# Trunk layer on one core: the q, k, v, o and z projections as seven half-size products (Strassen's scheme), all heads ahead of attention

## The chip, the cores and the metric

The kernel runs on one core of one Trainium2 chip. The metric is device time in microseconds (us) of one execution; lower is better. The median of three runs of the kernel before is 2274.1 us.

## The reference, cut to what matters

One layer of a hybrid trunk, for 1024 prompt tokens and for 32 sample tokens (8 sequences of 4), model width 1024. The part that the change touches is the product of the normalised rows with the columns of `w_in` that give q, k, v, o and z (each 2048 columns, four heads of 512), and the chunkwise attention that reads them:

```python
h = rmsnorm(x, norm_w)
pool_in, pool_z, qk_pre, v, o_pre, m_z, if_pre, gate_pre = jnp.split(h @ w_in, SPLIT_OFFSETS, axis=-1)
...
qk, conv_hist_new = causal_conv_silu(qk_pre, conv_hist, conv_w, conv_b)
q, k = jnp.split(qk, 2, axis=-1)
hc, c, n, m = mlstm_chunkwise(heads(q), heads(k) * (HEAD_DIM ** -0.5), heads(v), ...)
hc = hc * jax.nn.sigmoid(o_pre)
hc = head_rmsnorm(hc, mlstm_norm_w)
bm = (hc * jax.nn.silu(m_z)) @ w_mlstm_down
g_a, g_b = jnp.split(jax.nn.sigmoid(gate_pre), 2, axis=-1)
x = x + (g_a * a + g_b * bm) @ w_out
```

`mlstm_chunkwise` runs, for each head, over eight chunks of 128 tokens; from chunk to chunk it carries a 512 x 512 memory `C` (with one more column for the normaliser). The outputs are the layer's rows and all its new states.

## The kernel before

Every float32 product is made of three products of split operands: an operand x becomes `hi` (rounded, by ACT, L75 and L77) and `lo` = x - `hi` (by DVE, L81 and L83), and `mm3` (L88 to L90) adds hi x hi, hi x lo and lo x hi on PE.

The order of the work is as follows.

1. `norm_in` normalises the rows and leaves them feature-major as `hh` and `hl`, 1056 tokens wide (1024 of the prompt, then the 32 of the sample).
2. `head_gemm(h)`, for the four heads in turn, makes the products. For q and k the weights stand and the tokens move in three chunks of 352 columns (`fm`, 24 matmuls for a tile of 128 features and a chunk); `qk_tile` then does the causal convolution (three DVE operations, L488), silu, and a store to DRAM. For v, o and z the tokens stand and 256 weight columns move (`tok_group`). The sample's 32 rows take part in the q and k products as moving columns; for v, o and z they are separate float32 matmuls (`few`, L129). `load_w` loads 512 KB of weights at a time into `wraw` (2 buffers) and splits them into `whi` and `wlo` (3 buffers each).
3. `attn(h)` is a generator of eight `attn_step`s. While `head_gemm(h+1)` is written out, `tick` takes a step of it after each unit of product, at a rate of 0.45. So a head's attention is traced between the next head's products. The gates of all heads run in the same way beside head 0's products.
4. The last head's attention, and then `sample` (32 parts, each loads and stores 1 MB of state `ct`), run beside the merge gates (`merge_gates`, products of `hh` with the `gate_pre` columns) and the pool branch (`pool_branch`), at rates of 1.0 and 1.5. Then follow the down projections, `w_out` and the tail.

One `attn_step` of a middle chunk does on PE: 4 score matmuls (L605), 4 transposes of k (L629), 6 matmuls of the weighted scores with v and 24 of q with `C` (both into `num`), 24 for the new memory (eight groups of three into `kv`, which has two buffers), and 4 transposes of the result (L662). On DVE it does: `vlo`, the gated q (`t2k`, L618), `ql`, the decayed scores `p` (L607), `pl`, `kl`, eight updates of `C` (L642), four `Cl` (the split of the new `C`), and `den` (L651), its reciprocal (L652), the row sum `rs_ms` (L96), and the two products on the result (L654, L659): 23 operations. `Ch` and `Cl`, the split memory that the 24 q matmuls of the next chunk read, have one buffer each. The first chunk of a head has no q matmuls (and no gated q and no `ql`); the last makes no `Ch` and `Cl`. The loads of a step (`qk`, `v`, `dg`, `o`, `zz`) are issued by SP.

The kernel is built by a scheduler that sets the order of the instructions within each engine's queue from the traced program; an engine then runs its queue strictly in that order, and waits on semaphores.

```python
            self.feed(self.attn(h), 0.45)
...
        self.feed(rest(), RATE_A)
        self.merge_gates(range(5))
```

Of the kernel before, what the change touches and what calls it, by code (L numbers as in the profile page):

```python
# [18 lines left out]
P = 128  # L19
D = 1024  # L20
T = 1024          # prompt tokens
DB, DS = 8, 4     # sample batch, sample tokens
# [7 lines left out]
CW = NT // 3      # token chunk of the feature-major products  # L30
# [3 lines left out]
PH = 15           # pooling history  # L34
# [12 lines left out]
RATE_G, RATE_A, RATE_S = 0.8, 1.0, 1.5  # L47


class Trunk:  # L50
# [5 lines left out]
    # ---------------------------------------------------------------- helpers  # L56
# [35 lines left out]
    def rstd(self, pool, ss, n, rows=P):  # L92
        """(ss / n + eps) ** -0.5, one value per partition"""
        nc = self.nc
        ms = self.t(pool, [P, 1], "rs_ms", bufs=3)
        nc.vector.tensor_scalar(out=ms[:rows], in0=ss, scalar1=1.0 / n, scalar2=EPS, op0=ALU.mult, op1=ALU.add)  # L96
        r = self.t(pool, [P, 1], "rs_r", bufs=3)
        nc.gpsimd.tensor_tensor(out=r[:rows], in0=ms[:rows], in1=self.mhalf[:rows], op=ALU.pow)  # L98
        return r[:rows]

    def load_w(self, ap, n, scale=None):
        """rows of a weight, 256 columns at most: list of (hi, lo) for each k-tile"""
# [3 lines left out]
        for k0 in range(0, kt, 4):  # L106
            kk = min(4, kt - k0)
            raw = self.t(self.wp, [P, 4, 256], "wraw", bufs=2)
# [15 lines left out]
    def few(self, ps, rows, w):  # L124
        """NS rows (feature-major tiles, float32) times a weight: four partial sums, one per column group"""
# [5 lines left out]
    def sum4(self, out, ps, pool, groups=4):  # L131
        """sum of the partial sums of few()"""
# [9 lines left out]
    def fm(self, w, f, mov, consume, chunks=range(3)):  # L142
        """out[f-tile, tokens]: the weights stand, the activations (list of (hi, lo) [P, NT]) move"""
# [13 lines left out]
    def feed(self, gen, rate):  # L157
        """trace gen alongside the products: rate of its parts for each unit of product"""
# [16 lines left out]
    # ---------------------------------------------------------------- phase A  # L175
    def consts(self):
# [7 lines left out]
        nc.vector.memset(self.ones, 1.0)  # L184
        self.vc = self.t(c, [P, 72 + P], "vcols")
        self.nw = self.vc[:, 0:8]

    def columns(self):
        """per-feature vectors as columns"""
# [6 lines left out]
        v1 = self.t(self.ap_, [64, P], "v1")  # L196
        for o, n, name in ((8, 8, "ple_norm_w"), (16, 8, "pool_scale"), (24, 16, "mlstm_norm_w"), (40, 32, "conv_b")):
            nc.sync.dma_start(v1[o - 8:o - 8 + n, :], I[name].rearrange("(a b) -> a b", b=P))
        v2 = self.t(self.ap_, [P, P], "v2")
# [6 lines left out]
    def masks(self):  # L206
        nc, c = self.nc, self.cp
        one = self.t(self.ap_, [P, P], "one")
        nc.gpsimd.memset(one, 1.0)
        tri = self.t(self.ap_, [P, P], "tri")    # 1 where t >= s  # L210
# [14 lines left out]
        self.sel = self.t(c, [P, NS], "sel")     # 1 where the partition is t modulo 32  # L225
        nc.vector.tensor_reduce(out=self.sel, in_=self.ident.rearrange("p (g t) -> p t g", g=4), axis=AX.X,
                                op=ALU.add)
        # 1 / min(t + 1, 16)
        cnt = self.t(self.ap_, [P, 16], "cnt")
# [4 lines left out]
    def histories(self):  # L234
        """the rows before the convolution, feature-major"""
        nc, I, c = self.nc, self.I, self.cp
        self.chist = self.t(c, [P, 32, 24], "chist")
        h1 = self.t(self.ap_, [24, 2 * M], "h1")
        nc.sync.dma_start(h1, I["state_conv"].rearrange("b j f -> (b j) f"))
        for f0 in range(0, 32, 16):  # L240
            ps = self.mmps()
            for f in range(16):
                nc.tensor.transpose(ps[:, f * 24:(f + 1) * 24], h1[:, (f0 + f) * P:(f0 + f + 1) * P],
                                    self.ident[:24, :24])
            nc.vector.tensor_copy(self.chist[:, f0:f0 + 16, :], ps[:, :384].rearrange("p (f r) -> p f r", r=24))

    def norm_in(self):
# [3 lines left out]
        hp = self.hp  # L251
# [4 lines left out]
        v0 = None  # L256
        for i0, n in ((0, 3), (3, 3), (6, 3)):
            xs = []
            for i in range(i0, i0 + n):
                rows = P if i < 8 else NS  # L260
                x = self.t(self.ap_, [P, D], "x", bufs=6)
                nc.sync.dma_start(x[:rows], I["x_prompt"][i * P:(i + 1) * P, :] if i < 8 else I["x_sample"])
                xs.append((x, rows))
            if v0 is None:
                v0 = self.t(self.ap_, [8, P], "v0")
                nc.sync.dma_start(v0, I["norm_w"].rearrange("(a b) -> a b", b=P))
                ps = self.mmps()
                nc.tensor.transpose(ps[:, :8], v0, self.ident[:8, :8])
                nc.vector.tensor_copy(self.nw, ps[:, :8])
            for i, (x, rows) in enumerate(xs, i0):  # L270
                junk = self.t(self.ap_, [P, D], "xj", bufs=2)
                ss = self.t(self.ap_, [P, 1], "xss", bufs=3)
                if i % 3 == 1:
                    nc.vector.scalar_tensor_tensor(out=junk[:rows], in0=x[:rows], scalar=1.0, in1=x[:rows],
# [985 lines left out]
```

## Time and profile before

| what | value |
| --- | --- |
| runs of the kernel | 2271.71, 2274.1, 2277.27 us; median 2274.1 |
| the profiled execution | span 2277.1 us, 3.0 above the median |
| PE busy | 2235.1 us, 98% of the span, 16282 matmuls |
| DVE busy | 1121.0 us, 49% |
| ACT busy | 853.4 us, 37% |
| POOL busy | 126.4 us, 6% |
| traffic with HBM | 135 GB/s over the span |

PE, DVE, ACT and POOL are the four compute engines, SP issues the DMAs, PEld is PE's weight load. "Busy" is time in which an instruction was under way. A matmul's duration contains its drain, and the next one starts before it ends; so the price of a matmul in a stream is the distance from its start to the next one's start.

### The profile page before, as it was taken

The page shows a single profiled execution, that of the slowest core. Times are in us where ns is not written, and L with a number is a line of the kernel's source. Part 1 is how long each engine was busy: PE and PEld are TensorE (multiplying, and loading weights), DVE is VectorE, ACT ScalarE, POOL GpSimd, SP SyncE. Part 2 cuts the span into 40 slices and gives each one's busy share as a digit, 9 for nine tenths or more (in the row PEclk, how much of TensorE's full clock was granted, in tenths as well). Part 3 has the DMA queues.
Part 4 walks back from the last instruction along what each step waited for, and adds up shares of the span by engine and source line. Part 5 has one row for each costly group of instructions (what it writes and reads, how often), then busy time and mean ns, then how long its engine had stood idle before and what let it go on. Part 6 is the DMA issues. An engine that isn't in the chain of part 4 may idle for free.

```text
span 2277.1 us, 39798 instructions
## 1 busy us (share of the span) xinstructions
PE 2235.1 (98%) x16282; PEld 2137.3 (94%) x16282; DVE 1121.0 (49%) x2143; ACT 853.4 (37%) x1707; POOL 126.4 (6%) x380
## 2 busy tenths in 40 slices
PE   7999999999999999999999999999999999999998
PEld 6989999999999999999999998877878999999998
DVE  6551157444475343764434554567554234543545
ACT  5552255333354333553333332222233331223443
POOL 2120011000010000100000000000000000000100
PEclk8999999999999999999999999999999999999999
DMA  4353333344343344334444443777678333323112
GB/s 139 105 158 114 102 105 112 116 127 131 108 125 119 107 124 132 122 115 123 116 140 120 137 128 106 237 268 256 247 264 290 127 109 117 104 86 123 52 47 82
DMA packets 249866, 309.81 MB, mean 136 GB/s; under 512 B 14726, under 2 KB 187102, under 8 KB 249660
## 3 DMA queue, kind: packets, MB, share of 16 engines
q1 hardware_dynamic: 249684, 307.27, 42.3%
q8 instruction: 128, 2.10, 0.4%
q14 instruction: 54, 0.44, 0.1%
HBM read 198.17 MB, written 109.40 MB: 135 GB/s over the span
## 4 chain that ended last, share of the span: by engine, by line
PE 91%; DMA 5%; DVE 2%; ACT 1%; issue 1%; SPq 0%; DVEq 0%; POOL 0%; POOLq 0%; ACTq 0%
PE mm L88 25%; PE mm L89 25%; PE mm L90 25%; PE mm L129 2%; PE num L88 2%; PE num L89 2%; PE num L90 2%; PE num L774 1%; PE kv L88 1%; PE kv L90 1%; PE kv L89 1%; DMA ct<-state_mlstm_C 1%; PE misc L605 1%; DMA new_C_sample<-ct 1%; PE kv L778 1%; DMA draw<-hcD 1%
## 5 line engine op out<-in xcount | busy, mean ns | idle before, releaser
L88 PE MATMUL mm<-hh,whi 128*128 128x352 f32 x1536 | 502.8, 328 | 5.1 <-ACT whi L75 3.9
L89 PE MATMUL mm<-hl,whi 128*128 128x352 f32 x1536 | 499.1, 325 | 0.0
L90 PE MATMUL mm<-hh,wlo 128*128 128x352 f32 x1536 | 497.4, 325 | 0.0
L89 PE MATMUL mm<-wlo,hh 128*128 128x256 f32 x1536 | 433.0, 282 | 0.0
L88 PE MATMUL mm<-whi,hh 128*128 128x256 f32 x1536 | 432.6, 283 | 0.0
L90 PE MATMUL mm<-whi,hl 128*128 128x256 f32 x1536 | 430.8, 281 | 0.0
L81 DVE TENSOR_TENSOR wlo<-wraw,whi 128x1024 fp32r<-128x1024 f32 (+1 forms) x136 | 162.6, 1196 | 350.5 <-ACT whi L75 347.8
L88 PEld LDWEIGHTS mm<-hh,whi 128*128 128x128 f32 x1536 | 291.1, 190 | 15.9 <-ACT whi L75 4.2
L89 PEld LDWEIGHTS mm<-hl,whi 128*128 128x128 f32 x1536 | 292.1, 190 | 6.1 <-issue 5.0
L90 PEld LDWEIGHTS mm<-hh,wlo 128*128 128x128 f32 x1536 | 291.1, 190 | 6.2 <-issue 5.0
L88 PEld LDWEIGHTS mm<-whi,hh 128*128 128x128 f32 x1536 | 288.2, 188 | 8.6 <-ACT ph L75 4.9
L90 PEld LDWEIGHTS mm<-whi,hl 128*128 128x128 f32 x1536 | 290.2, 189 | 0.0
L89 PEld LDWEIGHTS mm<-wlo,hh 128*128 128x128 f32 x1536 | 288.3, 188 | 0.0
L75 ACT ACTIVATE whi<-wraw 128x1024 fp32r<-128x1024 f32 (+1 forms) x136 | 140.3, 1032 | 210.9 <-PE mm L89 98.1
L488 DVE SCALAR_TENSOR_TENSOR acc<-z,vcols,acc 128x352 f32<-128x352 f32 (+1 forms) x288 | 168.6, 590 | 81.0 <-ACT acc L486 75.5
L642 DVE SCALAR_TENSOR_TENSOR C<-C,dec,kv 128x258 f32<-128x258 f32 x224 | 102.0, 478 | 78.2 <-PE kv L90 77.1
L779 DVE SCALAR_TENSOR_TENSOR ct<-ct,dec,kv 128x512 f32<-128x512 f32 x128 | 91.8, 744 | 95.0 <-PE kv L778 94.1
L90 PE MATMUL mm<-mvhB,wlo 128*128 128x352 f32 x384 | 122.9, 321 | 0.3 <-DVE wlo L83 0.3
L88 PE MATMUL mm<-mvhB,whi 128*128 128x352 f32 x384 | 122.7, 323 | 0.4 <-ACT whi L77 0.3
L89 PE MATMUL mm<-mvlB,whi 128*128 128x352 f32 x384 | 122.9, 321 | 0.0
L98 POOL TENSOR_TENSOR rs_r<-rs_ms,cst 128x1 f32<-128x1 f32 (+1 forms) x60 | 38.8, 647 | 1058.1 <-DVE rs_ms L96 1021.4
L81 DVE TENSOR_TENSOR Cl<-C,Ch 128x516 fp32r<-128x516 f32 x112 | 77.7, 693 | 30.0 <-ACT Ch L75 27.8
(333 smaller groups left out, 4042.8 us busy)
## 6 DMA issues: line engine op xcount, KB each, us to landing
wraw<-w_in SPq DMA_DIRECT2D x112, 512.0 KB
ct<-state_mlstm_C SPq DMA_DIRECT2D x32, 1024.0 KB
new_C_sample<-ct SPq DMA_DIRECT2D x32, 1024.0 KB
qkD<-qkout SPq DMA_DIRECT2D x32, 512.0 KB
qk<-qkD SPq DMA_DIRECT2D x32, 512.0 KB
sgD<-sz SPq DMA_DIRECT2D x16, 528.0 KB
sg<-sgD SPq DMA_DIRECT2D x16, 528.0 KB
x<-x_prompt SPq DMA_DIRECT2D x16, 512.0 KB
```

Source lines behind the costliest of these rows:

```text
L75: self.nc.scalar.activation(out, in_, AF.Copy)
L81: self.nc.vector.tensor_tensor(out=out, in0=in_, in1=hi.bitcast(F32), op=ALU.subtract)
L88: mm(ps, lhsT=sh, rhs=mh, start=start, stop=False)
L89: mm(ps, lhsT=sh, rhs=ml, start=False, stop=False)
L90: mm(ps, lhsT=sl, rhs=mh, start=False, stop=stop)
L98: nc.gpsimd.tensor_tensor(out=r[:rows], in0=ms[:rows], in1=self.mhalf[:rows], op=ALU.pow)
L129: self.nc.tensor.matmul(ps[g, :], lhsT=rows[:, k, :], rhs=w[k][2], start=k < 4, stop=k >= kt - 4)
L488: nc.vector.scalar_tensor_tensor(out=acc[:, :tot], in0=z[:, o:o + tot], scalar=wc(o), in1=acc[:, :tot], op0=ALU.mult, op1=ALU.add)
L605: nc.tensor.matmul(ps[:, :L], lhsT=qk[:, 4 + d, :], rhs=qk[:, d, :], start=d == 0, stop=d == 3)
L642: nc.vector.scalar_tensor_tensor(out=self.C[:, d, x, :n], in0=self.C[:, d, x, :n], scalar=self.dec[:, h * NCH + c, 0:1], in1=kv[:, :n], op ...
L774: nc.tensor.matmul(num[32 * d:32 * d + 32, 0, :], lhsT=qm[:, b * P + d * NS:b * P + (d + 1) * NS], rhs=ct[:, d, :], start=b == 0, stop=b = ...
L779: nc.vector.scalar_tensor_tensor(out=ct[:, d, :], in0=ct[:, d, :], scalar=self.dec[:, h * DB + b, 1:2], in1=kv, op0=ALU.mult, op1=ALU.add)
```

## The change

q, k, v, o and z of one head are now made in blocks of 512 columns (20 blocks in all). The 1024 prompt tokens, the 1024 rows of the weight and the 512 columns are each cut in half; the block is then a 2 x 2 by 2 x 2 product of matrices, which takes eight half-size products in the plain way and seven by Strassen's scheme (in Winograd's form), with sums of operands ahead and sums of results behind.

- `norm_in` also builds the sums of the token side, once for all blocks: `T3`, `M2` and `N4` (each 4 tiles of 128 x 512, split), and it leaves a sum `M1` in the late half of `hh` and `hl`. `plain_h` puts the plain rows back there after the last block, since the merge gates and the pool branch read them. The callback `first` places the first two half products of the first block between the two halves of `norm_in`.
- `split_block` makes the seven half products. For each block DVE adds four pairs of weight tiles (128 x 1024), and does two `s2` adds, two negated adds and six adds in `put`; ACT copies two banks to `s1`. Seven weight tiles are split in place of four.
- In a half product (`half_product`) of q or k, 24 matmuls move 512 token columns each; of v, o or z, 48 matmuls move 256 weight columns each. The counts over the kernel: 2304 matmuls of 352 columns become 1344 of 512; 4608 of 256 become 4032.
- The sample's rows are separate float32 matmuls for all five kinds now (`few_part`, 16 for a block, 320 in all, where 192 were for v, o and z), with 32 small sums for q and k.
- The convolution of a tile runs over 512 and 568 columns in place of 352, 352 and 376.
- `run` traces all 20 blocks first, then the gates, and then the attention of all heads and the sample, at a rate of 2.6 (2.1 for the sample), beside the merge gates. What of the attention is left after seven of the eight groups of merge gates is traced on its own.

The diff, cut to its core:

```diff
-RATE_G, RATE_A, RATE_S = 0.8, 1.0, 1.5
+RATE_A, RATE_S = 2.6, 2.1
+HT = T // 2
...
+    def half_product(self, banks, w, act, tok, start, stop):
+        (wh, wl), (ah, al) = w, act
+        mm = self.nc.tensor.matmul
+        for j, ps in enumerate(banks):
...
+                for k in range(4):
+                    for n, (st, mv) in enumerate(((sh, mh), (sh, ml), (sl, mh))):
+                        mm(out, lhsT=st[k], rhs=mv[k], start=start and opens and k == 0 and n == 0,
+                           stop=stop and k == 3 and n == 2, skip_group_check=True)
+    def split_block(self, w, c0, tok, to, stage=None, held=None):
...
+            self.half_product(a, self.split_w(r11), self.early[0], tok, True, False)
...
+                nc.scalar.activation(s1[-1], x, AF.Copy)
+            self.half_product(a, self.split_w(r12), self.early[1], tok, False, True)
...
+        add(x3, r11, r21)
+        add(r21, r21, r22)
+        add(r11, r11, r21)
+        b = two()
+        self.half_product(b, self.split_w(r11), ops["M2"], tok, True, False)
...
+        add(r12, r12, r11)
+        self.half_product(b, self.split_w(x3), ops["T3"], tok, False, True)
...
+        self.half_product(c, self.split_w(r22), ops["N4"], tok, True, True)
...
+        self.half_product(d, self.split_w(r21), ops["M1"], tok, True, False)
...
+        self.half_product(d, self.split_w(r12), ops["B22"], tok, False, True)
...
-            self.feed(self.attn(h), 0.45)
...
+        for h in range(H):
+            for kind in "qvkoz":
+                self.block(h, kind, held.pop() if held else None)
+        self.plain_h()
...
+            yield from gates
...
+            for h in range(H):
+                yield from self.attn(h)
...
-        self.merge_gates(range(5))
+        self.merge_gates(range(7))
+        while not _s:
+            next(self.bg)
```

How the change moves instructions shows at two places of the queues.

On PE, in the attention of a head: before, the eight groups of `kv` stand between matmuls (`mm`) of the next head's products. This is a piece of head 0's attention in the queue of before:

```order
L88 MATMUL mm_3990<-hh_135,whi_3697 128x352
L89 MATMUL mm_3990<-hl_136,whi_3697 128x352
L88 MATMUL kv_3896<-vhi_421_3087,kh_3880 128x258
L89 MATMUL kv_3896<-vlo_422_3088,kh_3880 128x258
L90 MATMUL kv_3896<-vhi_421_3087,kl_3881 128x258
L88 MATMUL kv_3901<-vhi_421_3087,kh_3880 128x256
L89 MATMUL kv_3901<-vlo_422_3088,kh_3880 128x256
L90 MATMUL kv_3901<-vhi_421_3087,kl_3881 128x256
L90 MATMUL mm_3990<-hh_135,wlo_3698 128x352
L88 MATMUL mm_4026<-hh_135,whi_3691 128x352
```

And this is PE's queue of the change where a step of head 1 ends and the next begins (L833 are the transposes of the result, L776 the scores, L800 the transposes of k; `ph`, `pl` are the weighted scores):

```order
L90 MATMUL kv_11663<-vlo_1238_9501,kh_11618 128x256
L91 MATMUL kv_11663<-vhi_1237_9500,kl_11619 128x256
L833 MATMUL misc_11683<-ident_112,t2k_11674 128x128 x4
L776 MATMUL misc_11704<-qk_11691 128x128 x4
L800 MATMUL misc_11752<-ident_112,qk_11691 128x128 x4
L89 MATMUL num_11715<-vhi_1237_9500,ph_11711 128x258
L90 MATMUL num_11715<-vlo_1238_9501,ph_11711 128x258
L91 MATMUL num_11715<-vhi_1237_9500,pl_11712 128x258
L89 MATMUL num_11715<-vhi_1237_9500,ph_11711 128x256
```

The `mm` rows are gone from it. From its row 7150 to its row 8449, PE's queue holds the 24 steps of heads 1, 2 and 3, one after the other, and no matmul of any other work; the 14 tiles of the first seven groups of merge gates (1008 matmuls) stand ahead of them, around the gates and the eight steps of head 0.

On DVE, in the attention of a middle chunk: before, the operations of the step stand among weight splits (`wlo`) and the convolution (`acc`) of the next head:

```order
L642 SCALAR_TENSOR_TENSOR C_3092<-C_3092,dec_1206,kv_10876 128x258
L642 SCALAR_TENSOR_TENSOR C_3092<-C_3092,dec_1206,kv_10881 128x256
L618 TENSOR_TENSOR t2k_11190<-qk_11159,dg_11163 128x512
L81 TENSOR_TENSOR wlo_11423<-wraw_11420,whi_11422 128x1024
L81 TENSOR_TENSOR Cl_3094<-C_3092,Ch_3093 128x516
L81 TENSOR_TENSOR ql_11193<-t2k_11190,qh_11192 128x512
L488 SCALAR_TENSOR_TENSOR acc_11026<-z_11019,vcols_134,acc_11026 128x376
L642 SCALAR_TENSOR_TENSOR C_3092<-C_3092,dec_1206,kv_10888 128x258
L642 SCALAR_TENSOR_TENSOR C_3092<-C_3092,dec_1206,kv_10893 128x256
L488 SCALAR_TENSOR_TENSOR acc_11026<-z_11019,vcols_134,acc_11026 128x376
```

Now only operations of the attention stand there (L813 updates `C`, L830 is the last product on the result, `t2k` on L789 is the gated q; the last five rows belong to the next chunk, except the `Cl` between them, the fourth of this one):

```order
L830 SCALAR_TENSOR_TENSOR t2k_12650<-t2k_12650,rs_r_12656,zz_12536 128x512
L813 SCALAR_TENSOR_TENSOR C_9505<-C_9505,dec_9163,kv_12634 128x258
L813 SCALAR_TENSOR_TENSOR C_9505<-C_9505,dec_9163,kv_12639 128x256
L82 TENSOR_TENSOR Cl_9507<-C_9505,Ch_9506 128x516
L82 TENSOR_TENSOR vlo_1238_9501<-v_12749,vhi_1237_9500 128x2x256
L789 TENSOR_TENSOR t2k_12778<-qk_12747,dg_12751 128x512
L82 TENSOR_TENSOR Cl_9507<-C_9505,Ch_9506 128x516
L778 SCALAR_TENSOR_TENSOR p_12765<-misc_12760,dg_12751 128x128
L82 TENSOR_TENSOR ql_12781<-t2k_12778,qh_12780 128x512
L82 TENSOR_TENSOR pl_12768<-p_12765,ph_12767 128x128
```

What moved: the weight splits and the convolution are ahead of all of it, and a step's `vlo`, gated q, `p`, `ql` and `pl` stand behind the last updates of `C` of the step before.

## Rows read from the trace of the kernel before

**Rows 1.** The page: busy time, share of the span and instructions of each engine.

```profile
PE 2235.1 (98%) x16282; PEld 2137.3 (94%) x16282; DVE 1121.0 (49%) x2143; ACT 853.4 (37%) x1707; POOL 126.4 (6%) x380
```

**Rows 2.** Windows: length, busy of PE, PEld, DVE, ACT, POOL, clock, DMA share, GB/s.

```profile
0.00:57.00 57.00, 42.70 (x238) 39.05 (x239) 36.96 (x86) 30.41 (x55) 13.52 (x31) 0.85 0.44 138
342.00:399.00 57.00, 57.00 (x392) 56.87 (x391) 41.19 (x80) 30.36 (x66) 8.45 (x31) 1.00 0.35 111
1425.00:1767.00 342.00, 331.16 (x1918) 275.91 (x1917) 198.71 (x344) 99.86 (x181) 11.70 (x35) 1.00 0.76 263
```

**Rows 3.** Timeline (start, us, engine, line): matmuls of 352 and 512; sample's rows.

```profile
1424.35 0.33 PE L89 MATMUL mm<-hl,whi 128*128 128x352 f32 x1
1424.51 0.63 PE L778 MATMUL kv<-vst,km 96*128 96x512 f32 x2
...
1424.98 0.33 PE L90 MATMUL mm<-hh,wlo 128*128 128x352 f32 x1
...
239.64 1.07 PE L129 MATMUL mm<-wraw,hs 128*32 128x256 f32 x16
```

**Rows 4.** DVE by line and shape: count, busy us, mean ns, idle before.

```profile
L81 DVE TENSOR_TENSOR wlo<-wraw,whi 128x1024 fp32r<-128x1024 f32 x128 | 157.1, 1228 | 346.1 <-ACT whi L75 343.4 <-PE mm L90 2.0
L488 DVE SCALAR_TENSOR_TENSOR acc<-z,vcols,acc 128x352 f32<-128x352 f32 x192 | 111.4, 583 | 65.5 <-ACT acc L486 61.7 <-POOL z L477 0.8
L81 DVE TENSOR_TENSOR Cl<-C,Ch 128x516 fp32r<-128x516 f32 x112 | 77.7, 693 | 30.0 <-ACT Ch L75 27.8
L659 DVE SCALAR_TENSOR_TENSOR t2k<-t2k,rs_r,zz 128x512 f32<-128x512 f32 x32 | 24.0, 749 | 11.3 <-POOL rs_r L98 11.3
L81 DVE TENSOR_TENSOR vlo<-v,vhi 128x512 fp32r<-128x512 f32 x32 | 22.1, 690 | 10.0 <-ACT vhi L75 8.2
L607 DVE SCALAR_TENSOR_TENSOR p<-misc,dg 128x128 f32<-128x128 f32 x32 | 9.3, 290 | 22.8 <-PE misc L605 22.8
```

**Rows 5.** PE by line and shape: scores and result's transposes, all steps.

```profile
L605 PE MATMUL misc<-qk 128*128 128x128 f32 x256 | 34.0, 276 | 0.0
...
L662 PE MATMUL misc<-ident,t2k 128*128 128x128 f32 x128 | 20.2, 272 | 0.5 <-DVE t2k L659 0.5
```

**Rows 6.** Timeline, head 3's last chunk, its tail with no other work on PE.

```profile
1377.92 0.28 PE L89 MATMUL num<-Cl,qh 128*128 128x256 f32 x1
...
1378.04 0.28 PE L90 MATMUL num<-Ch,ql 128*128 128x256 f32 x1
...
1378.60 0.48 DVE L642 SCALAR_TENSOR_TENSOR C<-C,dec,kv 128x258 f32<-128x258 f32 x1 [5.48 <-PE kv L90]
...
1383.51 0.48 DVE L642 SCALAR_TENSOR_TENSOR C<-C,dec,kv 128x256 f32<-128x256 f32 x1
1383.90 0.29 DVE L720 TENSOR_TENSOR qg<-qs,gS 128x128 f32<-128x128 f32 x1
```

**Rows 7.** Windows: 117 to 124.4 (head 0), 1378 to 1384 (end of attention).

```profile
117.00:121.00 4.00, 0.15 (x1) 0.16 (x2) 4.00 (x16) 3.94 (x7) 4.00 (x1) 1.00 0.64 184
121.00:124.40 3.40, 3.40 (x13) 3.40 (x14) 3.31 (x8) 3.39 (x4) 3.03 (x5) 0.51 0.78 275
...
1378.00:1384.00 6.00, 4.45 (x28) 3.36 (x27) 5.10 (x14) 0.89 (x3) 1.67 (x4) 1.00 0.29 102
1440.00:1450.00 10.00, 10.00 (x54) 7.56 (x55) 5.72 (x9) 2.25 (x3) 0.00 (x0) 1.00 1.01 372
```

**Rows 8.** The gates' first store and the first decay matrix loaded, on SP.

```profile
68.01 0.28 SPq L324 DMA_DIRECT2D g8D<-g  x1
...
126.23 1.15 SPq L588 DMA_DIRECT2D dg<-DD  x1
```

**Rows 9.** SP's waits in the sample stage: total us, times, longest us.

```profile
SPq L772 <- DMA new_C_sample<-ct: 105.1, 26, 8.6
```

**Rows 10.** Timeline of POOL: the same copy ahead of a convolution, twice.

```profile
116.44 4.64 POOL L472 COPY z<-zc 128x3 f32<-128x3 f32 x1 [8.85 <-DVE acc L488]
...
71.65 0.18 POOL L472 COPY z<-zc 128x3 f32<-128x3 f32 x1
```

More of the change, by code (lines that the diff above doesn't have):

```diff
@@ new lines, in norm_in @@
+        self.columns()
+        first()
+        xs = xsamp[:, 0, :]
+        nc.sync.dma_start(xs[:NS], I["x_sample"])
+        norm(8, xs, NS)
+        ps = self.mmps()
+        for k in range(KT):
+            nc.tensor.transpose(ps[:, k * NS:(k + 1) * NS], xs[:NS, k * P:(k + 1) * P], self.ident[:NS, :NS])
+        v = ps[:, :KT * NS].rearrange("p (k t) -> p k t", t=NS)
+        nc.vector.tensor_tensor(out=self.hs, in0=v, in1=self.nw.unsqueeze(2).to_broadcast([P, KT, NS]), op=ALU.mult)
+        self.hi(self.hh[:, :, T:], self.hs)
@@ new lines, in norm_in @@
+        part = lambda x, k0, s: [x[:, k, s] for k in range(k0, k0 + 4)]
+        early = slice(0, HT)
+        self.ops = dict(B11=(part(self.hh, 0, early), part(self.hl, 0, early)),
+                        B21=(part(self.hh, 4, early), part(self.hl, 4, early)),
+                        B22=(part(self.hh, 4, late), part(self.hl, 4, late)),
+                        M1=(part(self.hh, 0, late), part(self.hl, 0, late)),
+                        T3=[[x[:, k] for k in range(4)] for x in t3],
+                        M2=[[x[:, k] for k in range(4)] for x in m2], N4=n4)
@@ L565, in attn_setup, with block @@
+        return To()
+    def block(self, h, kind, held=None):
+        off = {"q": O_Q, "k": O_K, "v": O_V, "o": O_O, "z": O_Z}[kind] + h * DH
+        to = self.qk_block(h, kind == "q") if kind in "qk" else self.tok_block(kind, h)
+        self.split_block(self.I["w_in"], off, kind in "voz", to, held=held)
     def attn_setup(self):
@@ new lines, in run, with first @@
+        self.xp, _x = self.pool("sums", "right")
+        self.wp, _w = self.pool("weights1")
+        self.gp, _g = self.pool("gemm")
+        self.nraw, self.nsb = 6, 6
+        held = []
+        def first():
+            early = lambda x, k0: [x[:, k, :HT] for k in range(k0, k0 + 4)]
+            self.early = [(early(self.hh, 0), early(self.hl, 0)), (early(self.hh, 4), early(self.hl, 4))]
+            held.append(self.split_block(self.I["w_in"], O_Q, False, None, stage=0))
+        self.norm_in(first)
@@ L1195, in run @@
-        _g.close()
+        next(gates)
         self.pp, _p = self.pool("gates2")
         _s = []
-        last = self.bg
         def rest():
-            yield from last
+            yield from gates
+            _a.close()
+            self.atp, _at = self.pool("attn", "right")
+            self.attn_setup()
+            for h in range(H):
+                yield from self.attn(h)
             _at.close()
```

469 lines of the change are left out of this document (282 added, 187 removed).

## The prediction

> **What bounds the kernel now.** I read the page's busy shares first, then windows by stage, then the distances between matmuls, and last the single rows on which the change rests. PE is busy 98% of the span and DVE 49% [rows 1]: where PE has a full queue, the time is the sum of its matmuls, and removing matmuls is worth their distance. The stretch of 342 to 399 us, head 1's products with head 0's attention between them, shows why: PE is busy all 57 us while DVE has 41 us of work and ACT 30 [rows 2]. Whatever DVE and ACT do there is hidden, since PE always finds a ready matmul of the products. Only the start (43 of 57 us busy) and the sample stage (331 of 342) leave PE idle [rows 2]. So I ask two things: what the shorter products save, and what now hides the latencies that they hid.
>
> I take the profiled execution's 2277.1 us as base; it is 3.0 above the median, and I take 3 off at the end.
>
> **The matmuls.** A matmul of 352 columns takes .16 us from start to start (1424.35 to 1424.51), and two of 512 take .47 (1424.51 to 1424.98), .235 each [rows 3]; one of 256 takes .12 (1377.92 to 1378.04) [rows 6].
> - q, k: 2304 x .16 = 369 us become 1344 x .235 = 316: 53 less. The larger piece per matmul eats half of the saving, because one of 512 columns costs 1.47 times one of 352, and the sample's columns move to separate matmuls.
> - v, o, z: 4608 become 4032, 576 x .12 = 69 less; I take 68.
> - Sample rows: 8 float32 matmuls (16 records) take 1.07 us [rows 3], so 128 more cost 17, and the 32 small sums 1: 18 more.
>
> Together 103 us less. This is all that the change gives on PE. The Trainium skill ("TensorE: Matmul & The Clock Gate", "Back-to-back issue gap") puts a matmul of 512 columns in a long stream at about 131 ns; the trace disagrees, with .235. By the page's figure q and k would take 1344 x .131 = 176 us, an estimate from that page, and the saving would be 140 us larger.
>
> **The start.** The sums on the token side are DVE work ahead of the third half product: for each of four feature tiles four sums and three more `lo` of 512 columns, 2 at .75 and 5 at .69 [rows 4], 4 x 4.95 = 20 us. The two early half products (48 matmuls, 11 us) stand beside them, but also beside the normalisation of the late tokens, which is there already. I take 14 more idle us, between 5 (the 11 hide their share) and 25 (nothing hides, and ACT's `hi` come on top).
>
> **Waits within the blocks.** A q or k block has on PE 168 x .235 + 2 = 41.6 us. On DVE it has 7 splits and 4 pair adds of 1024 columns at 1.23, 24 convolution operations of 512 or 568 columns at about .79 (scaled from .583 for 352 and the .75 of L659 for 512), and ten operations of 512 at .69 to .75 [rows 4]: 13.5 + 19 + 7 = 39.5 us. That is 95% of PE's time, where the stretch of head 1 had 72% [rows 2]. The seven products also hang on each other through the adds of weights and the banks. A v, o or z block has some 21 us of DVE work in 41: no wait. I take 10 us for the eight q and k blocks, between 0 and 60 (each block waiting for DVE by 7).
>
> **plain_h and the gates.** The five operations for each of four tiles that restore the late tokens (some 4 x 3.5 = 14 us of DVE [rows 4]) stand between the last block and the merge gates of the late tokens; the early chunk can go first: 4 us, between 0 and 10. From the gates' store to the first loaded decay matrix it takes 58 us [rows 8], hidden now under head 0's products. In the changed queue merge gates stand there: 5 us, between 0 and 15.
>
> **The attention without cover.** This term decides. The changed PE queue holds 24 steps of heads 1, 2 and 3 with no other matmul between them; the merge gates that the text puts beside them stand ahead, around head 0. PE's own work in a middle step is 54 x .12 = 6.5 us, 1.06 for the scores (34.0 / 32) and .63 for each of two sets of transposes [rows 5], less the drains that overlap: 8.3 us. The 24 q matmuls read `Ch` and `Cl`, which DVE and ACT make from the step's last updates of `C`. How long that takes without other work shows in the tail of head 3's last chunk: the last q matmul starts at 1378.04, the first update of `C` at 1378.60, and the last ends, for the next operation, at 1383.90 [rows 6]: 5.86 us, although PE had kv groups ready. That last chunk makes no `Cl`. A middle step adds, on the same engine, four `Cl` and then `vlo`, gated q, `ql`, `p` and `pl` ahead of the next q matmuls. DVE operations overlap by .09 (.48 lasting, .39 apart [rows 6]), so these are 4 x .60 + 3 x .60 + 2 x .20 = 4.6 [rows 4]. Then PE does six matmuls on the weighted scores (.7) and the 24 on `C` (2.9). The sum is 5.86 + 4.6 + 3.6 = 14.1 us for a step. The first chunk of a head has no q matmuls, gated q or `ql` (10.0), the last no `Cl` (11.7): 6 x 14.1 + 21.7 = 106.3 us a head, against 8 x 8.3 - 2.9 = 63.5 of PE work. The 42.8 between are idle time; for three heads 128 us.
>
> Bounds: below, DVE alone sets the pace. Its 23 operations are 8 x .48 for `C`, 4 x .69 for `Cl`, three of .69, three of .75, two of .29 and three of one column (.5 for them together, an estimate from the .29), 12.0 us, less 23 x .09: 9.9. A head is then 75.6 us and the idle time 3 x 12 = 36. Above, nothing overlaps: 12.0 + 2.9 + .7 + .4 for the first kv group + .6 for one ACT pass on the way: 16.6, and 3 x 63 = 188.
>
> **The clock.** At 117 to 121 PE did nearly nothing, and in the next 3.4 us the granted clock was .51 [rows 7], the lower of its two levels (1.2 of 2.4 GHz). In 1378 to 1384, where PE was busy 4.45 of 6 us with pauses between kv groups, it stayed at 1.00 [rows 7]. A bare step is more like the second, with pauses ahead of the scores. At the lower level the PE part of a step's chain (2.9 + .7 + .4) would double, 4 us. I take 10 us in all, between 0 and 40.
>
> **The sample.** 2.1 parts for each unit of product in place of 1.5 asks for more traffic: it ran at 263 GB/s with a DMA share of .76 [rows 2], which makes about 346 at full share, and SP already waited 105 us in it for a `ct` buffer's store [rows 9]. The 64 MB cannot be packed much tighter: I take 10 us, between 0 and 40.
>
> **The sum.** -103 + 14 + 10 + 4 + 5 + 128 + 10 + 10 = +78: 2355 by the profile's base, 2352 as a median.
>
> **The rivals.**
> - *DVE's pace, and so faster.* If the chain through `Cl`, the scores and q overlaps from step to step, so that a bare step lasts 9.9 us, the idle time is 36 in place of 128 and the clock costs nothing: -103 + 33 + 36 + 10 = -24, a median of 2250. The point from which it decides: without the clock term the rest sums to -60, which allows 20 idle us a head, or a step of 11.2 us. For it speaks that DVE work of 12 us a step is the largest single item; against it, that `Ch` and `Cl` have one buffer, that the q matmuls need all of `ql`, and that `vlo`, gated q, `p` and `ql` stand behind the last `C` in DVE's queue. Chance .11.
> - *Blocked copies on POOL.* A 3-column copy ahead of a convolution took 4.64 us at 116.44 and .18 at 71.65 [rows 10]; at 116.44 DVE was busy without a pause [rows 7]. In the q and k blocks DVE is at 95%, and four such copies stand on each block's path: if one in each costs 4.6, 37 us more, 2389. The Trainium skill ("SBUF — State Buffer", "Terms") says that DVE and GpSimd share one port pair, held for a whole instruction. By that rule such copies wait in all eight blocks; the trace bears it out in one row. Chance .12.
> - *The sample bound by its transfers*, 30 us more: 2382. Rows 9 speak for it, the DMA share of .76 against it. Chance .08.
> - *The lower clock in each bare step*: 24 x 4 less the 10 counted, 2438. The window 1378 to 1384 speaks against it. Chance .07.
> - *The 512-column matmul costs as little as one of 352* when weights come from a steady stream: 1344 x .075 = 101 less, 2251. Rows 3 speak against it. Chance .03.
>
> **How the numbers follow.** The forecast, about 14 us a bare step, has the remaining chance of .59; its time is 2352. Its own terms between their bounds reach from about 2275 (all of them low, with steps near 12) to 2440. The range of 2280 to 2430 takes in the rivals on the slow side but for the last part of the clock's, and leaves out the two that end at 2250. A measurement of this kernel tells 0.3%, 7 us, from no change. Faster by more than that has the two rivals and .02 of the forecast's lower end: .16. Within it .05, slower .79.
>
> **What would show it.** In the changed profile: q and k matmuls .235 apart and v ones .12 (if less, the first term is too small); PE about full in the blocks, its waits there on DVE's `wlo` or adds; a stretch of some 320 us behind the merge gates in which PE is busy about 60% and its idle time ends on DVE's `ql`, `Cl` or `C`; scores of neighbouring steps about 14 us apart. Scores 10 us apart, or merge gates found between them, would make the forecast wrong; so would a start with PE idle for over 60 us.

## The result and the profile after

The changed kernel takes 2494.59 us (median of 4 runs, 2494.3 to 2500.44) against 2274.43: 1.097 times the time of before, with a 95% interval of 1.0955 to 1.0986. It is slower, as forecast, but by 220 us where 78 were forecast, and outside the range.

The page of the changed kernel, busy time by engine (against [rows 1]):

```profile
PE 2249.2 (90%) x15066; PEld 2013.8 (81%) x15066; DVE 1391.1 (56%) x2386; ACT 890.6 (36%) x1586; POOL 173.1 (7%) x348
```

PE's share fell from 98% to 90%. To see where, I cut both traces at the same marks (first gates matmul, first score, first score of head 1, first sample matmul, first down projection) and subtract from each stretch its matmuls at the distances of a full stream (.16, .234, .118 and .12 us for 352, 512, 256 and 258 columns). What remains is idle time and low clock; the last row ends at the last matmul:

| stretch | before: us beyond the matmuls | after: length | after: us beyond the matmuls |
| --- | --- | --- | --- |
| products to the gates (before: to the sample, with gates and attention among them) | 45.9 of 1386 | 1007.4 | 151.9 |
| gates to the first score | (in the first row) | 61.2 | 6.5 |
| attention of head 0, beside the merge gates | (same) | 192.9 | 3.4 |
| attention of heads 1 to 3 | (same) | 325.0 | 136.8 |
| sample, pool branch, last merge gates | 36.2 of 380 | 397.7 | 94.2 |
| the rest | -0.3 | 499.3 | 2.3 |

The sum beyond the matmuls rises by 313.3 us and the matmuls fall by 97.9: the 215.4 between the two spans (2492.6 and 2277.1). Windows of the changed kernel (length, busy of PE, PEld, DVE, ACT, POOL, clock, DMA share, GB/s) show the three places:

```profile
102.00:340.00 238.00, 223.90 (x1534) 196.81 (x1533) 136.47 (x161) 87.65 (x123) 26.29 (x56) 0.96 0.28 91
340.00:345.00 5.00, 1.27 (x16) 0.49 (x8) 4.61 (x5) 2.84 (x4) 0.00 (x0) 1.00 0.20 63
345.00:350.00 5.00, 3.46 (x21) 2.62 (x22) 3.65 (x5) 1.33 (x2) 0.00 (x0) 0.58 0.57 166
1069.00:1261.00 192.00, 191.70 (x1328) 191.12 (x1326) 98.17 (x190) 69.70 (x135) 4.40 (x8) 0.99 0.46 145
1262.00:1586.00 324.00, 239.09 (x1609) 204.76 (x1608) 237.27 (x538) 137.37 (x274) 14.31 (x27) 0.98 0.45 128
...
1587.00:1984.00 397.00, 345.31 (x1925) 271.69 (x1919) 204.53 (x379) 100.62 (x184) 14.06 (x40) 0.92 0.66 226
```

**The blocks.** The 102 to 340 window is one head's five blocks: PE is idle in it for 14 us and runs at a mean clock of .96, while DVE is busy for 136 of 238 us. So DVE is not the bound. The timeline at the start of the next head's v block (start, us, engine, line) shows what happens in each v, o and z block:

```profile
339.73 1.04 PE L455 MATMUL misc<-wraw,hs 128*32 128x256 f32 x14
340.39 1.23 DVE L421 TENSOR_TENSOR wraw<-wraw,wraw 128x1024 f32<-128x1024 f32 x1 [5.83 <-PE misc L455]
...
342.14 1.21 DVE L421 TENSOR_TENSOR wraw<-wraw,wraw 128x1024 f32<-128x1024 f32 x1
...
343.38 2.95 ACT L76 ACTIVATE whi<-wraw 128x1024 fp32r<-128x1024 f32 x3 [0.50 <-DVE wraw L421]
...
344.49 0.51 PE L394 MATMUL mm<-whi,m2h 128*128 128x256 f32 x2 [3.72 <-ACT whi L76]
```

The weight add (L421) waits 5.83 us for the sample's matmul (L455), since it overwrites the tile that this one reads. Those matmuls stand in PE's queue behind the block's second product. So the third product's weights are added and split only when PE has nothing else: PE waits 3.72 us, and in the next 5 us its clock is .58 (the window 345 to 350). The waits of PE between 102 and 999 us (in total, times, longest), and the page's row of the adds:

```profile
PE mm L394 <- ACT whi L76: 42.9, 12, 3.7
PE misc L632 <- DMA part<-state_conv: 8.1, 7, 1.5
PE mm L394 <- DVE wlo L82: 6.4, 5, 1.3
```

```profile
L421 DVE TENSOR_TENSOR wraw<-wraw,wraw 128x1024 f32<-128x1024 f32 x80 | 97.7, 1221 | 129.6 <-PE misc L455 128.5
```

DVE waits in this way in 19 of the 20 blocks, but PE in 12 only: the v, o and z blocks, whose third product moves 256 weight columns (first row, 42.9 us of idle time). In the q and k blocks it moves 512 token columns and waits for nothing (second row):

```profile
L394 PE MATMUL mm<-whi,m2h 128*128 128x256 f32 x192 | 62.9, 338 | 42.9 <-ACT whi L76 42.9
...
L394 PE MATMUL mm<-m2h,whi 128*128 128x512 f32 x56 | 22.9, 409 | 0.0
```

The place of the sample's matmuls in PE's queue differs. In the v, o and z blocks 22 to 38 records of them stand directly ahead of the third product. In a q or k block at most four do, and the first 16 stand 8 us earlier, among the matmuls of the second product (at 289.03, the third product at 297.16).

**The bare attention.** Two scores of a middle step are 14.18 us apart (1436.62 and 1450.80), and between them the work passes from engine to engine. Timeline of the changed kernel, head 2:

```profile
1436.62 1.16 PE L776 MATMUL misc<-qk 128*128 128x128 f32 x8 [0.74 <-ACT t2k L835]
...
1438.46 0.69 DVE L82 TENSOR_TENSOR ql<-t2k,qh 128x512 fp32r<-128x512 f32 x1 [0.15 <-ACT qh L76]
1439.07 0.28 DVE L778 SCALAR_TENSOR_TENSOR p<-misc,dg 128x128 f32<-128x128 f32 x1
...
1439.41 0.66 PE L800 MATMUL misc<-ident,qk 128*128 128x128 f32 x4 [1.63 <-DVE p L778]
...
1443.81 0.17 ACT L821 ACTIVATE den<-num 128x1 f32<-128x1 f32 x1 [2.96 <-PE num L91]
1444.02 0.21 DVE L822 TENSOR_SCALAR den<-den,tok 128x1 f32<-128x1 f32 x1 [2.38 <-ACT den L821]
1444.19 0.48 DVE L813 SCALAR_TENSOR_TENSOR C<-C,dec,kv 128x258 f32<-128x258 f32 x1
...
1449.43 0.63 PE L833 MATMUL misc<-ident,t2k 128*128 128x128 f32 x4 [0.73 <-DVE t2k L830]
...
1450.80 1.16 PE L776 MATMUL misc<-qk 128*128 128x128 f32 x8 [0.73 <-ACT t2k L835]
```

DVE waits while PE does the q matmuls (`den`, 2.38 us), and PE waits while DVE does `vlo`, gated q, `Cl`, `ql` and `p`. A head takes 108 us (324 / 3), near the 106.3 of the prediction. The two longest rows among the waits of PE from 1262 to 1586:

```profile
PE misc L800 <- DVE p L778: 22.7, 24, 1.6
PE kv L89 <- DVE C L813: 22.0, 63, 0.5
```

**The sample's end.** The longest wait of the stage is a single one of 21.7 us, and the granted clock there is .50. In the 38 us before it, where the last parts stand, PE is busy for 23. The longest waits of PE from 1586 to 1984, the two windows, and the timeline:

```profile
PE mm L89 <- ACT sz L1084: 21.7, 1, 21.7
PE num L945 <- DMA ct<-state_mlstm_C: 13.6, 8, 2.8
```

```profile
1900.00:1938.00 38.00, 23.07 (x77) 10.11 (x76) 14.47 (x24) 4.80 (x8) 0.55 (x1) 0.67 0.78 285
1938.00:1960.00 22.00, 0.62 (x3) 0.19 (x1) 5.40 (x8) 6.81 (x11) 0.00 (x0) 0.50 0.34 104
```

```profile
1945.56 8.12 SPq L1102 DMA_DIRECT2D sz<-hcD  x4
1949.09 1.06 ACT L76 ACTIVATE mvhA<-sz 128x1024 fp32r<-128x1024 f32 x1 [6.51 <-DMA sz<-hcD]
...
1959.76 1.18 ACT L1084 ACTIVATE sz<-mm 128x352 f32<-128x352 f32 x3
1960.28 0.66 PE L89 MATMUL mm<-hh,whi 128*128 128x352 f32 x1 [21.66 <-ACT sz L1084]
```

The sigmoid of the last merge gates (L1084), for which PE waits, stands in ACT's queue behind four splits of loads (L1102) that are issued only at 1945.

### The profile page after: what moved, and what is told of

Read it like the earlier page. It is cut to its first block, busy times and chain, and to the rows that moved or that the text cites. A ratio compares the mean times of both kernels' runs of the same rounds, so it can differ in the third digit from the quotient of the medians.

```text
span 2492.6 us, 37772 instructions
## 1 busy us (share of the span) xinstructions
PE 2249.2 (90%) x15066; PEld 2013.8 (81%) x15066; DVE 1391.1 (56%) x2386; ACT 890.6 (36%) x1586; POOL 173.1 (7%) x348
## 4 chain that ended last, share of the span: by engine, by line
PE 78%; DVE 11%; DMA 6%; issue 2%; ACT 2%; SPq 1%; DVEq 0%; POOLq 0%; ACTq 0%; POOL 0%
PE mm L394 33%; PE mm L89 11%; PE mm L90 11%; PE mm L91 11%; DVE C L813 2%; DVE Cl L82 2%; PE misc L455 2%; DMA new_C_sample<-ct 2%; DVE wraw L421 2%; PE num L91 2%; PE num L945 1%; PE num L89 1%; PE num L90 1%; PE kv L949 1%; PE misc L800 1%
## 5 line engine op out<-in xcount | busy, mean ns | idle before, releaser
L89 PE MATMUL mm<-hh,whi 128*128 128x352 f32 x768 | 252.7, 329 | 23.3 <-ACT sz L1084 22.1
L90 PE MATMUL mm<-hl,whi 128*128 128x352 f32 x768 | 250.8, 327 | 0.0
L91 PE MATMUL mm<-hh,wlo 128*128 128x352 f32 x768 | 250.1, 327 | 0.0
L394 PE MATMUL mm<-whi,hl 128*128 128x256 f32 x768 | 216.7, 283 | 0.0
L394 PE MATMUL mm<-whi,hh 128*128 128x256 f32 x768 | 216.1, 283 | 0.0
L394 PE MATMUL mm<-wlo,hh 128*128 128x256 f32 x768 | 215.1, 281 | 0.0
L89 PEld LDWEIGHTS mm<-hh,whi 128*128 128x128 f32 x768 | 146.0, 190 | 31.7 <-ACT sz L1084 22.9
L421 DVE TENSOR_TENSOR wraw<-wraw,wraw 128x1024 f32<-128x1024 f32 x80 | 97.7, 1221 | 129.6 <-PE misc L455 128.5
L90 PEld LDWEIGHTS mm<-hl,whi 128*128 128x128 f32 x768 | 146.5, 191 | 7.7 <-issue 6.7
L91 PEld LDWEIGHTS mm<-hh,wlo 128*128 128x128 f32 x768 | 145.9, 190 | 8.3 <-issue 7.5
L394 PEld LDWEIGHTS mm<-whi,hl 128*128 128x128 f32 x768 | 144.4, 188 | 0.7
L813 DVE SCALAR_TENSOR_TENSOR C<-C,dec,kv 128x258 f32<-128x258 f32 x224 | 99.7, 475 | 50.0 <-PE kv L91 49.3
```

Source lines behind the costliest of these rows:

```text
L89: mm(ps, lhsT=sh, rhs=mh, start=start, stop=False)
L90: mm(ps, lhsT=sh, rhs=ml, start=False, stop=False)
L91: mm(ps, lhsT=sl, rhs=mh, start=False, stop=stop)
L394: mm(out, lhsT=st[k], rhs=mv[k], start=start and opens and k == 0 and n == 0, stop=stop and k == 3 and n == 2, skip_group_check=True)
L421: add = lambda o, x, y: nc.vector.tensor_tensor(out=o, in0=x, in1=y, op=ALU.add)
L813: nc.vector.scalar_tensor_tensor(out=self.C[:, d, x, :n], in0=self.C[:, d, x, :n], scalar=self.dec[:, h * NCH + c, 0:1], in1=kv[:, :n], op ...
```

## The experiments

Of the twelve, one is on the order, two on the blocks, two on the bare step, three on the sample, and four try a mixed version. e2, e4, e5, e9 and e11 were run once, the others two to six times. "Filler" is independent work that stands in a queue between dependent steps.

**The order alone.** Kernel of before, its `run` replaced by that of the change (no seven-product blocks):

```diff
-            self.feed(self.attn(h), 0.45)
...
+            yield from gates
...
+            for h in range(H):
+                yield from self.attn(h)
...
-        self.merge_gates(range(5))
+        self.merge_gates(range(7))
+        while not _s:
+            next(self.bg)
```

> The kernel before with its eight-product projections, but in the changed order: the products of all four heads first, then the gates, the attention and the sample beside seven groups of merge gates at the changed rates. Theory: the order is the loss. Three heads of attention without cover cost 138 us, the gates' start about 10, and the sample stage, which finds less filler, about 55: 2274 + 203 = some 2475 us. Rival: most of the loss lies in the blocks of seven products (waits on DVE), and the order costs only the bare attention and the gates: 2274 + 128 + 10 = some 2412 us.

Measured: 2464.09 us, 1.0831 of before (1.0799 to 1.0862). So the order alone costs 189 us. The same stretch of bare attention lies 139 us beyond its matmuls, the sample 88. The window of the bare attention:

```profile
1235.00:1562.00 327.00, 243.33 (x1610) 208.87 (x1609) 237.28 (x538) 137.45 (x275) 14.34 (x27) 0.96 0.44 127
```

PE and DVE are both busy about 73% of it, as in the changed kernel. The difference to the changed kernel, 30 us, is what the seven products cost on top: 98 us of matmuls are saved, 122 us more lie beyond them ahead of the gates (151.9 against 30.4), and the sample adds 6 (94 against 88).

**The sample's matmuls without the dependence.**

```diff
-                                      rhs=raw[k // 4][f][:, k % 4, :], start=k < 4, stop=k >= 4)
+                                      rhs=self.hs.rearrange("p k t -> p (k t)"), start=k < 4, stop=k >= 4)
```

> The changed kernel, with the sample's float32 matmuls reading a constant tile in place of the raw weights (so the sample's projections are left out; the matmuls remain, with as many columns). Theory: each block loses about 5 us because the adds of weight tiles overwrite tiles that the sample's matmuls still have to read, and these stand behind the second product on PE; without that dependence 20 blocks give back 3.5 to 4.5 us each, 70 to 90 us: some 2410 us. Rival: the wait is the chain of adds and splits on DVE and ACT itself, or the loads: at most 20 us, 2475 or more.

Measured: 2403.5 us, 91 less. The kernel leaves out the sample's projections, but the PE work is the same and only the reading of the raw tiles is gone. The list of PE's waits between 102 and 914 us shrinks to one row:

```profile
PE mm L394 <- DVE s L421: 0.2, 1, 0.2
```

The expectation spread the gain over 20 blocks. Since PE waited in 12, it is 7.6 us for each of these.

**The sample's matmuls early.**

```diff
+            if stage != 0:
+                r21, r22 = self.raw_w(w, c0, 1)
+                to.sample(((r11, r21), (r12, r22)))
             self.half_product(a, self.split_w(r12), self.early[1], tok, False, True)
```

> The changed kernel, with the second half of a block's weights loaded, and the sample's matmuls traced, ahead of the block's second product. Theory: the adds can then run under the second product (5.6 us); 50 to 80 us less, 2415 to 2445 us. Rival: the loads are not there in time with six buffers, the wait moves to the sample's matmuls: within 20 us of 2494.

Measured: 2401.38 us, 93 less, more than expected; 1.0555 of before (1.052 to 1.059). One head's blocks now run with PE full, at a clock of 1.00, and the add's wait for L458 (the former L455) is halved and hidden:

```profile
102.00:340.00 238.00, 237.23 (x1733) 213.51 (x1732) 150.91 (x177) 93.30 (x130) 25.67 (x57) 1.00 0.34 105
```

```profile
L424 DVE TENSOR_TENSOR wraw<-wraw,wraw 128x1024 f32<-128x1024 f32 x80 | 97.6, 1219 | 62.6 <-PE misc L458 61.5
```

With e2 this shows the cause of the blocks' wait: the overwritten weight tile, and the place of its reader in PE's queue. DVE's load is not it; it rose from 136 to 151 us a window and PE was busy for 237 of 238 us.

**The last merge gates ahead of the loads.**

```diff
+        self.merge_gates(range(7, 8))
         first = self.hc_tiles(self.pp, 0, "A", "sz")
-        self.merge_gates(range(7, 8))
```

> The changed kernel with the last group of merge gates traced ahead of the four loads of the attention's result (they were behind). Theory: the 21.8 us of idle PE at the sample's end go, since the sigmoid of the merge gates no longer stands behind the splits of loads that have not landed on ACT: 15 to 25 us less, some 2475. Rival: the loads' latency then stands ahead of the down projections in place of it: no change beyond 5 us.

Measured: 2481.83 us, 13 less, a little under what was expected: the stretch of the sample falls from 397.7 to 387.6 us and the rest by 5. The wait was real, but only half of its 21.7 us came off the stage; PE still waits 5.7 us there for the same operation on ACT.

**No low part of the memory.**

```diff
-                self.lo(self.Cl[:, d], self.C[:, d], self.Ch[:, d])
...
-                    self.mm3(o_, qh[:, d], ql[:, d], mh, ml, False, d == 3)
+                    nc.tensor.matmul(o_, lhsT=qh[:, d], rhs=mh, start=False, stop=False)
+                    nc.tensor.matmul(o_, lhsT=ql[:, d], rhs=mh, start=False, stop=d == 3)
```

> The kernel of e3_few_early (2401 us), with the low part of the memory left out of the q matmuls: no Cl, so 4 DVE operations and 8 of 24 q matmuls less in a step (the result is less exact). Theory: a bare step is a chain through DVE and PE in turn, so it loses 4 x .60 + 8 x .12 = 3.4 us, 13.6 to 10.2; over 21 steps of heads 1 to 3 some 70 us less, 2330. Rival 1: DVE alone sets the pace, 2.4 us a step, 50 us less. Rival 2: PE sets it, 1.0 us a step, 20 us less.

Measured: 2347.14 us, 54 less than e3. Two scores are now 11.35 us apart:

```profile
1402.90 1.16 PE L778 MATMUL misc<-qk 128*128 128x128 f32 x8 [0.74 <-ACT t2k L837]
...
1414.25 1.16 PE L778 MATMUL misc<-qk 128*128 128x128 f32 x8 [0.74 <-ACT t2k L837]
```

From 13.5 that is 2.15 less, below the chain's 3.4 and next to the 2.4 of DVE's pace. But DVE does not set the pace: the 12.0 us of its operations less four `Cl` of .69 [rows 4] are 9.2, or 7.5 with 19 overlaps of .09, in a step of 11.35. What the step lost is nearly the time of the four `Cl` in DVE's series; the .96 us of PE's shorter q matmuls did not show. That the chain now runs over ACT's last `Ch` instead is my reading of the queues, not shown.

**The merge gates spread over the steps.**

```diff
+            if self.spread is not None and self.spread > FREE and self.mark is not None:
+                self.nc.vector.tensor_copy(ps[:, 0:1], self.mark)
...
+        self.mark = den
```

> The kernel of e3_few_early, with the merge gates spread over the attention: a chunk of 24 matmuls (3.8 us) for each step, held back until that step's q matmuls are done, and 12 chunks left for the gates' chain. Theory: each step then takes about 14.5 to 15 us with 12.1 of PE work in it, where head 0 took 24 and the others 13.6: 32 x 14.8 = 474 in place of 520: some 2355 us. Rival: the chunk stands in PE's queue ahead of the next step's matmuls and lengthens the chain by its 3.8 us: 32 x 17.4 = 557, some 2440 us.

Measured: 2388.33 us, 13 less than e3, where 46 were expected. Head 0's steps fell to 16 us as meant, but those of heads 1 to 3 rose from 13.6 to 15.8. This lies between theory and rival: a chunk of 3.8 us in the queue cost the chain 2.2. Single steps ran at the low clock, as here, where the scores last 2.08 in place of 1.16 us. Over the stretch of heads 1 to 3 the granted clock is .97:

```profile
1212.55 2.08 PE L785 MATMUL misc<-qk 128*128 128x128 f32 x8 [0.69 <-ACT t2k L845]
```

```profile
1105.00:1484.00 379.00, 326.51 (x2211) 300.25 (x2211) 252.72 (x565) 148.65 (x304) 20.41 (x27) 0.97 0.45 132
```

The changed kernel has .98 in its bare steps and two such steps too (scores of 2.08 us at 1393.99 and of 2.07 at 1502.94). The clock is a small part of the 2.2: .03 of 379 us is 11 us, an estimate of at most .5 for each of 24 steps. That the rest is the chunk's place in the queue is argued, not shown.

**Filler kept for the sample**, at two paces of the sample (the second is the same with `RATE_S` 1.2 in place of 2.1):

```diff
-        self.merge_gates(range(7))
+        self.merge_gates(range(4))
...
+        self.merge_gates(range(4, 7))
         first = self.hc_tiles(self.pp, 0, "A", "sz")
```

> The kernel of e3_few_early (2401 us), with three of the seven groups of merge gates (69 us of matmuls) traced behind the pool branch, beside the sample, and four left for the attention. Theory: the sample stage has its own pace of some 390 us for 300 to 350 us of PE work, so 69 us more fit in with little added (388 to 410 us); the attention stage loses what head 0's steps had too much: 40 to 60 us less in all, some 2350 us. Rival: the sample stage grows by the 69 us and the attention becomes bare earlier: within 15 us of 2401.

Measured: 2408.82 us; the rival held in the total. The attention of head 0 fell by 44 us (193 to 148), but the sample stage grew by 52 (397 to 449). Its windows show why: the kept products ran after the sample's last part, and the sample itself still had PE idle and a low clock.

```profile
1700.00:1786.00 86.00, 71.92 (x318) 44.09 (x316) 51.82 (x88) 17.46 (x32) 3.53 (x9) 0.80 0.77 264
1786.00:1902.00 116.00, 107.17 (x637) 104.00 (x637) 26.73 (x46) 32.03 (x61) 0.55 (x1) 0.94 0.39 133
```

> The kernel of e9_filler_kept (2409 us) with the sample traced at 1.2 parts for each unit of product in place of 2.1, so that the three kept groups of merge gates stand between the sample's parts and not behind them. Theory: the sample stage's idle and low-clock time comes from products that stand behind the last part; beside it the stage falls from 449 to some 410 us (373 of PE work and the 36 of the kernel before): some 2370 us. Rival: the parts wait for their own transfers as before, no gain: within 10 us of 2409.

Measured: 2364.46 us, 44 less than e9. With the products between the parts the stage is 401 us, 34 beyond its matmuls (36 in the kernel before). The window holds the 401 and 6 us around them:

```profile
1453.00:1860.00 407.00, 390.69 (x2368) 336.64 (x2369) 217.20 (x395) 119.23 (x216) 13.27 (x40) 0.98 0.71 241
```

With 64 us more of matmuls in it (401 - 34 against 397.7 - 94.2) the stage is only 3 us longer than in the changed kernel. So products fit into the time that lay idle there. Whether the transfers set the length of some 400 us is not shown. The mean traffic of 226 GB/s was no limit, since 241 are reached here, but SP waits for the stores of `ct` in the changed kernel's stage for 125 us, against 105 in [rows 9]:

```profile
SPq L943 <- DMA new_C_sample<-ct: 125.0, 27, 9.3
```

**Two heads by seven products, two as before.** Since bare steps and a sample without products cost 195 us together, and the kernel frees the seven products' tiles before it allocates those of the attention, so that the two cannot stand side by side, I made heads 0 and 1 with the new blocks (and the early sample matmuls), then the plain rows, and heads 2 and 3 as before, with the gates and the attention between their products:

```diff
-        for h in range(H):
+        for h in range(NST):
             for kind in "qvkoz":
...
+        self.feed(rest(), RATE_P)
+        for h in range(NST, H):
+            self.head_gemm(h)
...
-        self.merge_gates(range(7))
+        self.merge_gates(range(5))
```

> Heads 0 and 1 by seven half products, with the sample's matmuls early; then plain rows, and heads 2 and 3 by the eight products of the kernel before, with the gates and the attention traced between them (0.9 parts for each unit of product), and the rest as in the kernel before. Theory: half of the matmul saving (49 us), 20 us of start and block waits and 8 of the transition against it, and no bare attention, since 476 us of products cover steps of 19 to 21 us: 2274 - 49 + 28 = some 2253 us. Rival: steps at 13 to 19 us spacing meet the chain of 14 us too often, or the sample stage lacks filler: 40 us more, 2290.

Measured: 2256.19 us, .9913 of before (.989 to .9936): .9% faster than the kernel before, and faster than the changed one. The page, and the windows of head 0's attention, of the others', and of the sample:

```profile
PE 2191.3 (97%) x15690; PEld 2054.5 (91%) x15690; DVE 1274.9 (57%) x2286; ACT 873.9 (39%) x1654; POOL 152.4 (7%) x364
```

```profile
596.00:761.00 165.00, 165.00 (x1411) 161.60 (x1412) 94.27 (x186) 70.76 (x135) 3.85 (x7) 1.00 0.47 136
761.00:1360.00 599.00, 598.34 (x4596) 590.89 (x4595) 345.35 (x683) 251.58 (x499) 33.22 (x91) 1.00 0.45 135
1360.00:1746.00 386.00, 373.19 (x2226) 313.80 (x2226) 210.08 (x387) 110.82 (x202) 13.83 (x40) 0.98 0.71 245
```

The attention is covered again: PE is full with the same steps.

> As e7_two_heads, with 0.75 parts for each unit of product; three steps of the last head then stand without matmuls between them and the merge gates are used up earlier. Theory: 3 bare steps cost 3 x 5.4 = 16 us and the sample some 10: about 25 us more than e7_two_heads. Rival: the wider spacing of the steps gives that back: within 5 us of it.

Measured: 2271.86 us (.9982, .9969 to .9994), 16 more than e7, where 25 were expected. The last head's stretch with its three bare steps lies 28 us beyond its matmuls, where e7 has 7.

> As e7_two_heads, with 0.82 parts for each unit of product (0.9 there, 0.75 in e8). Theory: between the two, since the last steps' cover is the difference: 2258 to 2268 us. Rival: the wider steps of heads 0 to 2 save more than the last ones lose: 2245 to 2253.

Measured: 2266.37 us (.9947, .9927 to .9967), between e7 and e8, as the theory has it.

> e7_two_heads (2256 us) with the sample at 1.2 parts for each unit of product in place of 1.5. Theory: as in e11, the later parts get products beside them, 36 us of excess fall to some 25: 2245 us. Rival: the sample's parts then end later than the products, and the tail is bare: 2260 or more.

Measured: 2267.7 us (.9947, .9929 to .9964). The rival held: the sample stage grew from 386 to 401 us, and its tail is bare. In its last 32 us (1730 to 1762) PE is busy for 18 at a clock of .61, where e7 has 30 of 31 us at 1.00 (1715 to 1746). e11 took the same pace with more products beside the sample.

## Why the prediction was partly right

- *The matmuls.* The forecast was -103, and -97.9 were found. In the changed kernel those of 512 columns are .234 apart in the median and those of 256 are .118. The figure of 131 ns from the Trainium skill ("TensorE: Matmul & The Clock Gate", "Back-to-back issue gap") is not borne out by this trace either, and the rival that rested on a cheap 512-column matmul falls.
- *The start.* The forecast was +14. In the first 102 us, 37 us lie beyond the matmuls, against 24 in the first 59 of before: +13.
- *Waits within the blocks*: the step that failed. I took 10 us, at most 60, from DVE's load against PE's, and for v, o and z "no wait". It came out the other way round: behind the start, PE waited for a block's weights in all 12 v, o and z blocks and in no q or k block. The wait is no matter of load. It is a dependence (the sample's matmul still has to read the tile that the add overwrites), which costs PE time where that matmul stands directly ahead of the third product. The 12 waits are 42.9 us of idle time, and behind each comes a stretch at the low clock. The excess ahead of the gates is 115 us after the start, less 22 in the stretch of before, which holds the gates and the attention too: 93. Removing the dependence gave back 91, moving its reader 93. To see it, I would have had to ask of each new in-place add who reads the tile before it and where that reader stands in PE's queue; the order of the changed kernel showed this.
- *plain_h and the gates.* The forecast was 9. There are 6.5 us to the first score, 3.4 in head 0, and 8 more at the end of the blocks, which are counted with the blocks: 18 in all.
- *The attention without cover.* The forecast was 128, with 14.1 us a step; 136.8 were found, with 13.5 and a head of 108 us. The 136.8 contain the low clock, for which I had 10 more, so 138 stand against them. The reading of the tail in [rows 6] held for the size, and part of that is luck: the first and the middle steps are shorter than forecast (9.5 and 13.5 against 10.0 and 14.1), the second and the last of a head longer (15.8 and 13.2 against 14.1 and 11.7; scores at 1464.4, 1477.6, 1487.1 and 1502.9). Of the three DVE operations on which I expected PE's idle time to end, only `C` has a long row (22.0 us); the longest is that of `p` (22.7). And e5 took 2.15 us off a step where the chain by my sum would lose 3.4. The rival of DVE's pace falls: DVE is busy 237 of 324 us, and a step takes 13.5 us and not 9.9.
- *The clock.* The forecast was 10 in the bare steps; their window has .98. The rival of the low clock in each step falls. Most of the low clock came elsewhere, behind the waits of the blocks and at the sample's end.
- *The sample*: the second step that failed. The forecast was 10, and 94.2 - 36.2 = 58 were found: 40 are matmuls that no longer stand in the stage (380 - 36.2 less 397.7 - 94.2), 18 its greater length. I priced its transfers alone, and not the products between its parts. The merge gates that had stood there were used up beside head 0, whose steps took 24 us on average (193 / 8) where a bare one took 13.5, so the stage's last parts stood bare and PE waited 13.6 us for loads of `ct`. And one queue order left PE idle for 21.7 us at its end. Filler that one stage takes is missing in the next: I counted that for heads 1 to 3 and not for the sample. The rival of the sample bound by its transfers is not settled.
- *Blocked copies on POOL.* This rival falls: none of the listed waits of PE in the blocks ends on POOL, and the copies of [rows 10] took .61 us in the mean in the blocks. The Trainium skill ("SBUF — State Buffer", "Terms") has DVE and GpSimd share one port pair; no wait of PE here shows it.

Summed: -98 + 13 + 93 + 10 (gates and head 0) + 137 + 58 + 2.6 (the rest) = 215.6, the 215.4 between the spans but for rounding.

## What to carry to other kernels

A saving in matmuls is worth its full size only while PE's queue holds enough independent products; ask for each stage of the new order which products stand between its dependent steps, and keep one account of them over all stages, since what the order uses early is missing late. Before making an in-place operation, look for the last reader of the tile and its place in its own engine's queue. A half-way version that keeps the cover (two heads by the new scheme, two by the old) may beat both ends.

## What the hardware showed that was not expected

The granted clock stayed at .98 on average in the bare steps, with PE busy 239 of 324 us in many short pieces. It fell to .50, the lower of its two levels, behind each of the 12 waits of PE in the v, o and z blocks, which lasted 3.3 to 3.7 us (1.00 at 340 to 345, .50 at 347 to 352). With what follows it, such a wait cost 7.6 us (the 91 us of e2 over 12), about twice its own length. With the merge gates spread over the steps (e6), PE was busy 327 of 379 us and the clock was .97. What sets the few steps at the low clock against the others, here and in e6, was not tried.
